# Key parts of an attention block: a buffer of their own for the low parts, fewer key transfers, block sums in smaller steps

## The chip, the core and the metric

The kernel runs on one core of a Trainium2 chip. Its time is the device time of one execution in microseconds (us); the number that counts is the median of several runs. Profiles are of one execution each, and a profiled execution has a time of its own.

Names used below: PE is TensorE, which multiplies matrices (PEld is its loading of weights); DVE is VectorE; ACT is ScalarE; POOL is GpSimd, which here does little but issue transfers; SP issues the other transfers. Each engine works its own list of instructions in order.

## What is computed

The reference is one layer of a generator over 512 latent tokens (an 8 x 64 grid) and 256 context tokens, of width 1024. `h` is the normalised, modulated input, `hc` the same for the context:

```
parts = _split_in(h @ w_in[i])                 # 10 parts of 1024 columns
q = _apply_rope(_heads(parts[4]), cos, sin)    # 16 heads of 64
k = _apply_rope(_heads(parts[5]), cos, sin)
v = _heads(parts[6])
k_c, v_c = ...                                 # hc @ w_in, key and value columns
attn = _neighbourhood_attention(q, k, v, k_c, v_c, rpb[i])
y_a = (silu(z_a) * b_gate * _dwconv3(c_gate * x_in, conv_w, conv_b)) @ w_out_conv
y_b = (silu(z_b) * attn) @ w_out_attn
x = x + gt * _rmsnorm((sigmoid(g_a) * y_a + sigmoid(g_b) * y_b) @ w_o[i], post_g)
```

Each token attends to a window of 8 x 16 latent keys and to all 256 context keys in one softmax.

## The kernel before

**Two parts per number.** Every product is made from float32 operands that are cut in two: a high part `H` (a cast on ACT, line 67) and a low part `L = source - H` (a subtraction on DVE, line 68). The helper `split` does both.

**The stages.** First the input is normalised and modulated into the tiles `h` (high and low part of each of eight 128-row pieces, lines 373 to 500), while the first products run (`steps`, lines 397 to 401). DVE's work there is the conditioning (line 352), `fL` (line 385) and the low parts of `h` (line 68). Convolution units and the context's conditioning follow, to about 117 us of the profile. Then come the keys and queries and the values of the first pair of heads, and then the attention: eight pairs of heads, each with two heads of four blocks, so 64 slots. In each slot the loop (lines 783 on) issues some of the fill work that `plan` lists for this pair (projections for later pairs, `qk`, `v`; convolution units `cx`, `bz`; gates `zb`, `g`), the gathering of the head before (`gather`, line 713 on PE), the scores of the block two slots ahead (`scores`, lines 663 and 672 on PE, 679 on DVE, 685 to 687 on ACT) and, every second slot, the transposes of two blocks (`turn2`, line 694) with the split into `TH` and `TL`. An output stage follows from about 527 us on.

**Products in seven instead of eight.** Some fill items are made by `pair` (lines 268 to 291): 256-column blocks, products at line 262, with sums of blocks in place of blocks. `pair` writes its two results into tiles of the tag `tc`, of which there are three in rotation: first `c1` (copy at line 273), then the second half of `c2` (line 276) and its first half (line 278). The two products after that accumulate into the bank that the copy at line 278 has read. In the pairs of heads 2, 4 and 6 of the plan, the items are `qk`, then `zb` by `pair`, then `cx` by `pair`. `Chunk.first` prepares the next chunk of weights for such an item: sums on DVE at lines 101, 103, 105 and 106, and splits.

**The block sums of h.** `pair` needs sums of blocks of `h`: `S2`, `S3`, `S4`, `X1`. `block_sums` (lines 561 to 579) makes them once, in four steps (k = 0 to 3), each of two tiles `a` and `b` of the tag `tc`: two additions (line 569), two half subtractions (570, 571), two half operations (573) and two splits into `S` tiles. The loop calls `next(sums)` in the slots 4, 6, 9 and 11.

**The keys.** `keys_queries(p)` projects queries and keys of a pair. `keys` (lines 631 to 636) splits the keys into high and low part, once for the 512 latent and once for the 256 context columns. The low part goes into a tile `low`, also of the tag `tc`. Then three transfers on POOL's queue put the parts where the scores need them: high half to the second tile (634), low half to the second tile (635), low half over the high half in the first tile (636, which must wait until 634 has read it). The two tiles `ks` of a pair are for its head 0 and head 1; four buffers hold two pairs.

**What sets the order.** The order of instructions on each engine is set by a scheduler that takes the program's order and puts in what it holds to be ready, as buffers of a tag come free. The first stage is written under a fixed order for its own instructions, but others can stand between them.

Of the kernel before, what the change touches and what calls it, by code (L numbers as in the profile page):

```python
# [10 lines left out]
F32R = mybir.dt.float32r  # L11
# [4 lines left out]
P = 128  # L16
D = 1024
KT = 8
S = 512
C = 256  # L20
# [7 lines left out]
def layer(ctx: ExitStack, tc, xp, ctxt, ctxT, cc, wmod, small, wfirst, win, wout, wo, rel, tab, out):  # L28
    nc = tc.nc
# [4 lines left out]
    cv = ctx.enter_context(tc.tile_pool(name="cv", bufs=2))  # L34
# [29 lines left out]
    def split(H, L, src, scale=None):  # L64

        if scale is None:
            nc.scalar.copy(H, src)  # L67
            nc.vector.tensor_sub(L, src, H.bitcast(F32))  # L68
        else:
            nc.scalar.mul(H, src, scale)  # L70
            nc.vector.scalar_tensor_tensor(
                out=L, in0=src, scalar=scale, in1=H.bitcast(F32), op0=ALU.mult, op1=ALU.subtract
            )
# [91 lines left out]
    def proj_c(ps, w, u):  # L165

        (H, L, _), cs = w, slice(u * P, (u + 1) * P)
        for k in range(KT):
            nc.tensor.matmul(  # L169
                ps, lhsT=H[k][:, cs], rhs=hcs[k].rearrange("p a c -> p (a c)"), start=k == 0, stop=False,  # L170
                skip_group_check=True,
            )
        for k in range(KT):
            nc.tensor.matmul(
                ps[:, :C], lhsT=L[k][:, cs], rhs=hc[0][k], start=False, stop=k == KT - 1, skip_group_check=True
            )

    def summed(ps):
        t = cv.tile([P, S], F32, name="ta")[:, :256]
        nc.scalar.copy(t, ps[:, 256:])  # L180
        nc.vector.tensor_add(t, t, ps[:, :256])
        return t
# [137 lines left out]
    def unit(w, i, m=hx):  # L320
        ps = pj()
        proj_T(ps, w, i, m)
        return ps


    with ExitStack() as p0:
# [17 lines left out]
        cols = {}  # L344
# [204 lines left out]
        ks = [5, 6, 7, 0, 1, 2, 3, 4]  # L549
# [11 lines left out]
    def block_sums():  # L561

        h0, h1 = slice(0, 256), slice(256, S)
        for n in ("S2", "S3", "S4", "X1"):
            blocks_h[n] = [], []
        for k in range(4):
            a, b = (cv.tile([P, S], F32, name="tc", bufs=3) for _ in range(2))
            for x, i in ((a, k), (b, 4 + k)):
                nc.vector.tensor_add(x, hx[0][i].bitcast(F32), hx[1][i].bitcast(F32))
            nc.vector.tensor_sub(b[:, h1], b[:, h1], a[:, h1])  # L570
            nc.vector.tensor_sub(a[:, h1], a[:, h0], a[:, h1])
            for o, x, y in ((a[:, h0], b[:, h1], a[:, h0]), (b[:, h0], a[:, h0], b[:, h0])):
                nc.vector.scalar_tensor_tensor(out=o, in0=x, scalar=-1.0, in1=y, op0=ALU.mult, op1=ALU.subtract)
            for x, names, tag in ((a, ("S2", "S3"), f"u{k}"), (b, ("S4", "X1"), ("a2", "a3", "s0", "s1")[k])):
                t = hp.tile([P, 2, S], F32R, name=f"{names[0]}{k}", tag=tag)
                split(t[:, 0], t[:, 1], x)
                for n, ts in zip(names, (h0, h1)):
                    for y in range(2):
                        blocks_h[n][y].append(t[:, y, ts])
            yield  # L580
# [4 lines left out]
    aw = pa.enter_context(tc.tile_pool(name="aw", bufs=2, reuse_waits="tile"))  # L585
    swap = [(i + 16) % 32 for i in range(32)]
    lo, hi = slice(0, 64), slice(64, P)
# [5 lines left out]
    def rope(ps, turn=0):  # L593
        t1 = cv.tile([P, S], F32, name="ta")
        nc.vector.tensor_mul(t1, ps, cosin[:, 0])
        t2 = cv.tile([P, S], F32, name="tb")
        nc.vector.stream_shuffle(t2, ps, swap)
        nc.vector.tensor_mul(t2, t2, cosin[:, 1])
        if not turn:
            nc.vector.tensor_add(t1, t1, t2)  # L600
            return t1
        t3 = cv.tile([P, S], F32, name="ta")
        nc.vector.tensor_add(t3[:, :S - turn], t1[:, turn:], t2[:, turn:])
        nc.vector.tensor_add(t3[:, S - turn:], t1[:, :turn], t2[:, :turn])
        return t3
# [16 lines left out]
    def keys_queries(p):  # L622
        w = chunk()
        qf = rope(unit(w, 0), 64)
        sc = 0.125
        qd, qe = ([aw.tile([P, S], F32R, name=n, bufs=3) for h in range(2)] for n in ("qd", "qe"))
        split(qd[0], qe[0], qf, sc)
        yield
        ks = [aw.tile([P, S + C], F32R, name="ks", bufs=4) for h in range(2)]

        def keys(src, cols):
            low = cv.tile([P, S], F32R, name="low", tag="tc", bufs=3)[:, :cols.stop - cols.start]
            split(ks[0][:, cols], low, src)
            nc.gpsimd.dma_start(ks[1][lo, cols], ks[0][hi, cols])
            nc.gpsimd.dma_start(ks[1][hi, cols], low[hi])
            nc.gpsimd.dma_start(ks[0][hi, cols], low[lo])

        keys(rope(unit(w, 1)), slice(0, S))
        yield
        ps = pj()  # L640
        proj_c(ps, w, 1)
        keys(summed(ps), slice(S, S + C))
        for t in (qd, qe):
            for o in (lo, hi):
                nc.gpsimd.dma_start(t[1][o], t[0][hi])  # L645
            nc.gpsimd.dma_start(t[0][hi], t[0][lo])
        KQ[p] = qd, qe, ks
        yield
# [41 lines left out]
    def turn2(pts, b, TH, TL):  # L690
        tps = [psT().rearrange("p (c q) -> p c q", c=4) for _ in pts]
        for tp, pt in zip(tps, pts):
            for c in range(4):
                nc.tensor.transpose(tp[:, c], pt[:, c * P:(c + 1) * P], ident)  # L694
        for n, tp in enumerate(tps):
            split(TH[:, b + n], TL[:, b + n], tp)

    def gather(p, h, TH, TL):
        r, q = (lo, hi)[h], (hi, lo)[h]
        if h == 0 and p % 2 == 0:  # L700
            t = hp.tile([P, 2, S], F32, name=f"at{p}", tag=f"a{p // 2 % 2}")
            attn[p], attn[p + 1], attn[p, "both"] = t[:, 0], t[:, 1], t
        o = psO()
        o3 = o.rearrange("p (b q) -> p b q", b=4)

        work = [(4, slice(0, 4), lambda t: t[:, :, 2]), (5, slice(0, 4), lambda t: t[:, :, 3])]
        work.append((0, slice(0, 4, 3), lambda t: t[:, 0:4:3, 0]))
        for k in range(1, 3):
            work.append((k, slice(k - 1, k + 1), lambda t, k=k: t.rearrange("p b c q -> p (b c) q")[:, 4 * k - 3:4 * k + 1:3]))
        work.append((3, slice(2, 4), lambda t: t[:, 2:4, 1]))  # L710
        for n, (kt, dst, src) in enumerate(work):
            for t in (TH, TL):
                nc.tensor.matmul(  # L713
                    o3[:, dst], lhsT=V[p][:, kt, h], rhs=src(t),
                    start=n == 0 and t is TH, stop=n == len(work) - 1 and t is TL,
                )
        tmp = cv.tile([P, S], F32, name="ta")
        nc.scalar.copy(tmp[r], o[q])
        nc.vector.tensor_add(attn[p][r, 64:512], o[r, :448], tmp[r, :448])
        nc.vector.tensor_add(attn[p][r, 0:64], o[r, 448:], tmp[r, 448:])  # L720
# [38 lines left out]
    def chain(*gs):  # L759
        for g in gs:  # L760
            yield from g
# [6 lines left out]
    for g in (keys_queries(0), values(0)):  # L768
        for _ in g:
            pass  # L770
# [13 lines left out]
    pts = {n: scores(*blocks[n]) for n in range(2)}  # L784
    T = None
    sums = block_sums()
    done = 0
    for i, (p, h, b) in enumerate(blocks):
        slot = i % 8
        if slot == 0:  # L790
            items = chain(*(g for g, _ in fill[p]))
            total, done = sum(n for _, n in fill[p]), 0
        if i in (4, 6, 9, 11):
            next(sums)
        upto = -(-total * (slot + 1) // 8)
        while done < upto:
            next(items)
            done += 1
        if T is not None and b == 0:
            gather(*T)  # L800
        if i + 2 < len(blocks):
            pts[i + 2] = scores(*blocks[i + 2])
        if b == 0:
            TH = aw.tile([P, 4, 4, P], F32R, name="TH", bufs=1)
            TL = aw.tile([P, 4, 4, P], F32R, name="TL", bufs=1)
            T = p, h, TH, TL

        if b % 2:
            turn2([pts.pop(i - 1), pts.pop(i)], b - 1, TH, TL)
# [22 lines left out]
    for n, _ in enumerate(chain(merge_gates(2), merge_gates(3))):  # L832
        ks = range(4 * (n % 2), 4 * (n % 2) + 4)
# [205 lines left out]
    for i in range(2):  # L1039
        cols = slice(256 * i, 256 * (i + 1))  # L1040
# [92 lines left out]
```

## Time and profile before

| | us |
|---|---|
| median of 3 runs (725.94 to 729.69) | 726.06 |
| the profiled execution, its time | 731.14 |
| its span, first to last instruction | 729.3 |
| PE busy in the span | 708.0 |
| DVE busy | 586.8 |
| ACT busy | 425.3 |
| POOL busy | 49.9 |

The mean granted TensorE clock of the profiled execution is 0.987. Of a line of the profile, `L68` is line 68 of the kernel, `tc<-h` says what is written and what is read, `x24` how many instructions the line holds, and a bracket such as `[3.18 <-ACT tc L278]` says how long the engine had been idle before and what ended that.

### The profile page before, as it was taken

How to read it: one execution, taken by the hardware profiler on the slowest of the kernel's cores; microseconds unless marked ns; L12 is line 12 of the kernel's file. 1: busy time of each engine (PE TensorE's matmuls, PEld its weight loads, DVE VectorE, ACT ScalarE, POOL GpSimd, SP SyncE). 2: the span in 40 equal slices, each digit the busy share in tenths (PEclk: the TensorE clock that was granted, in tenths of full speed). 3: DMA queues.
4: the chain of work that ended last, by engine and by line, in shares of the span. 5: the costliest groups of instructions: out<-in, count | busy, mean ns of one | idle time of the engine just before them, and what ended most of it. 6: DMA issues, size and time to landing. Idle time of an engine off the chain costs nothing.

```text
span 729.3 us, 11059 instructions
## 1 busy us (share of the span) xinstructions
PE 708.0 (97%) x4052; PEld 621.7 (85%) x4052; DVE 586.8 (80%) x1139; ACT 425.3 (58%) x822; POOL 49.9 (7%) x102
## 2 busy tenths in 40 slices
PE   8999999999899989999899999899999999999996
PEld 5888888888788888898898899899989999988885
DVE  7979999569888877879687699799797765674996
ACT  7575642456476575775675675688774443352663
POOL 0000002030030300301201103000000000000000
PEclk9999999999999999999899999999999999999999
DMA  8986987362260533432553144232543333480013
GB/s 349 407 314 248 295 307 195 95 148 76 73 149 15 139 112 115 91 107 58 130 182 93 34 145 97 72 111 73 191 159 113 116 116 108 139 300 32 30 58 117
DMA packets 36825, 104.06 MB, mean 143 GB/s; under 512 B 4897, under 2 KB 6689, under 8 KB 36770
## 3 DMA queue, kind: packets, MB, share of 16 engines
q1 hardware_dynamic: 28946, 92.20, 36.8%
q0 software_dynamic: 7680, 11.02, 7.2%
q8 instruction: 32, 0.52, 0.3%
q14 instruction: 23, 0.19, 0.1%
q10 hardware_dynamic: 144, 0.13, 0.1%
HBM read 87.07 MB, written 5.24 MB: 127 GB/s over the span
## 4 chain that ended last, share of the span: by engine, by line
PE 59%; DVE 9%; DMA 5%; ACT 2%; issue 1%; POOL 1%; DVEq 0%; ACTq 0%; POOLq 0%; SPq 0%
PE ps L262 17%; PE ps L143 7%; PE ps L145 7%; PE ps L144 7%; PE ps L940 5%; PE ps L156 5%; PE ps L713 4%; DMA ks<-low 3%; PE ps L694 2%; PE ps L161 2%; DVE w L68 2%; PE ps L663 2%; DMA qe<-qe 1%; PE ps L169 1%; DVE TL L68 1%
## 5 line engine op out<-in xcount | busy, mean ns | idle before, releaser
L68 DVE TENSOR_TENSOR w<-raw,w 128x512 fp32r<-128x512 f32 (+1 forms) x170 | 146.1, 867 | 44.1 <-ACT w L67 43.4
L67 ACT CAST w<-raw 128x512 fp32r<-128x512 f32 (+1 forms) x170 | 128.5, 768 | 84.6 <-PE ps L145 31.4
L262 PE MATMUL ps<-S,w 128*128 128x256 f32 x768 | 102.8, 293 | 8.8 <-ACT tc L278 8.8
L262 PEld LDWEIGHTS ps<-S,w 128*128 128x128 f32 x768 | 99.3, 201 | 9.4 <-ACT tc L278 9.4
L143 PE MATMUL ps<-h,w 128*128 128x512 f32 x272 | 106.8, 392 | 0.0
L145 PE MATMUL ps<-h,w 128*128 128x512 f32 x272 | 106.2, 390 | 0.0
L144 PE MATMUL ps<-h,w 128*128 128x512 f32 x272 | 105.9, 389 | 0.0
L262 PE MATMUL ps<-h,w 128*128 128x256 f32 x576 | 75.2, 284 | 0.2 <-DVE g L279 0.2
L262 PEld LDWEIGHTS ps<-h,w 128*128 128x128 f32 x576 | 71.9, 191 | 1.5 <-DVE g L279 0.5
L145 PEld LDWEIGHTS ps<-h,w 128*128 128x128 f32 x272 | 51.1, 188 | 10.8
L143 PEld LDWEIGHTS ps<-h,w 128*128 128x128 f32 x272 | 51.2, 188 | 10.4
L144 PEld LDWEIGHTS ps<-h,w 128*128 128x128 f32 x272 | 51.1, 188 | 10.5
L685 ACT ACTIVATE pt<-ps,m 128x512 f32<-128x512 f32 x64 | 44.2, 691 | 17.8 <-DVE m L679 17.2
L687 ACT ACTIVATE pt<-pt,z 128x512 f32<-128x512 f32 x64 | 45.9, 726 | 9.0 <-DVE z L686 8.8
L67 ACT CAST TH<-ps 128x512 fp32r<-128x512 f32 x64 | 35.4, 587 | 18.5 <-PE ps L694 18.5
L68 DVE TENSOR_TENSOR TL<-ps,TH 128x512 fp32r<-128x512 f32 x64 | 43.1, 681 | 1.6 <-ACT TH L67 1.4
L679 DVE CUSTOM_DVE_ANT_1 ps<-ps,bt 128x512 f32<-128x512 f32 x56 | 38.8, 696 | 4.0 <-PE ps L663 4.0
L694 PE MATMUL ps<-ident,pt 128*128 128x128 f32 x256 | 33.7, 273 | 0.4 <-DVE TL L68 0.4
L645 POOL DMA_DIRECT2D qd<-qd x16 | 8.3, 524 | 356.7 <-issue 239.1
L156 PE MATMUL ps<-w,h 128*128 128x512 f32 x128 | 32.5, 395 | 0.0
L694 PEld LDWEIGHTS ps<-ident,pt 128*128 128x128 f32 x256 | 29.2, 140 | 3.1 <-ACT pt L687 0.9
L713 PE MATMUL ps<-TH,V 128*128 128x256 f32 (+1 forms) x96 | 29.9, 332 | 1.1 <-ACT TH L67 1.1
(247 smaller groups left out, 1377.3 us busy)
## 6 DMA issues: line engine op xcount, KB each, us to landing
raw<-in_win SPq DMA_DIRECT2D x74, 512.0 KB, 4.5
wm<-in_wmod SPq DMA_DIRECT2D x34, 512.0 KB, 6.2
raw<-in_wout SPq DMA_DIRECT2D x16, 512.0 KB, 3.6
bt<-in_rel SPq DMA_DIRECT2D x16, 256.0 KB, 3.3
B<-in_wo SPq DMA_DIRECT2D x8, 512.0 KB, 6.9
fraw<-in_wfirst SPq DMA_DIRECT2D x8, 384.0 KB, 8.5
qd<-qd POOLq DMA_DIRECT2D x24, 128.0 KB, 2.3
qe<-qe POOLq DMA_DIRECT2D x24, 128.0 KB, 3.8
```

Source lines behind the costliest of these rows:

```text
L67: nc.scalar.copy(H, src)
L68: nc.vector.tensor_sub(L, src, H.bitcast(F32))
L143: nc.tensor.matmul(ps, lhsT=H[k][:, cs], rhs=mH[k], start=k == 0, stop=False)
L144: nc.tensor.matmul(ps, lhsT=H[k][:, cs], rhs=mL[k], start=False, stop=False)
L145: nc.tensor.matmul(ps, lhsT=L[k][:, cs], rhs=mH[k], start=False, stop=k == KT - 1)
L156: nc.tensor.matmul(ps, lhsT=mH[k][:, ts], rhs=both[k].rearrange("p a c -> p (a c)"), start=k == 0, stop=False, skip_group_check=True,)
L262: nc.tensor.matmul(ps, lhsT=w[:, x, k], rhs=act[y][k], start=start and k + o == 0, stop=k == 3 and o == 2, skip_group_check=True,)
L679: nc.vector.tensor_tensor_reduce(out=s3, in0=s3, in1=bt[:, e::4 - e][:, 0:2], scale=-1.0, scalar=3.0e38, op0=ALU.add, op1=ALU.min, accum_o ...
L685: nc.scalar.activation(pt, s, AF.Exp, bias=m, scale=-1.0, accum_out=z)
L687: nc.scalar.mul(pt, pt, z)
L694: nc.tensor.transpose(tp[:, c], pt[:, c * P:(c + 1) * P], ident)
L713: nc.tensor.matmul(o3[:, dst], lhsT=V[p][:, kt, h], rhs=src(t), start=n == 0 and t is TH, stop=n == len(work) - 1 and t is TL,)
```

## The change

It does four things. The low parts of the keys get a tile of their own, `lows` (tag `kl`, one buffer, 768 columns), so the tag `tc` holds only block sums and the results of `pair`. The tiles `ks` have three buffers in place of four, so the second tile of a pair takes the buffer of the first tile of the pair before. The three key transfers are made once per pair over all 768 columns, after the context's keys are split, in place of once for each part: three in place of six. And `block_sums` gives way between the sums of a step and their splits, with eight calls in the slots 4, 5, 6, 8, 9, 10, 12, 13 in place of four.

```diff
@@ block_sums
             for o, x, y in ((a[:, h0], b[:, h1], a[:, h0]), (b[:, h0], a[:, h0], b[:, h0])):
                 nc.vector.scalar_tensor_tensor(out=o, in0=x, scalar=-1.0, in1=y, op0=ALU.mult, op1=ALU.subtract)
+            yield
             for x, names, tag in ((a, ("S2", "S3"), f"u{k}"), (b, ("S4", "X1"), ("a2", "a3", "s0", "s1")[k])):
@@ keys_queries
-        ks = [aw.tile([P, S + C], F32R, name="ks", bufs=4) for h in range(2)]
+        ks = [aw.tile([P, S + C], F32R, name="ks", bufs=3) for h in range(2)]
+        lows = aw.tile([P, S + C], F32R, name="kl", bufs=1)
 
         def keys(src, cols):
-            low = cv.tile([P, S], F32R, name="low", tag="tc", bufs=3)[:, :cols.stop - cols.start]
-            split(ks[0][:, cols], low, src)
-            nc.gpsimd.dma_start(ks[1][lo, cols], ks[0][hi, cols])
-            nc.gpsimd.dma_start(ks[1][hi, cols], low[hi])
-            nc.gpsimd.dma_start(ks[0][hi, cols], low[lo])
+            split(ks[0][:, cols], lows[:, cols], src)
 
         keys(rope(unit(w, 1)), slice(0, S))
         yield
         ps = pj()
         proj_c(ps, w, 1)
         keys(summed(ps), slice(S, S + C))
+        nc.gpsimd.dma_start(ks[1][lo], ks[0][hi])
+        nc.gpsimd.dma_start(ks[1][hi], lows[hi])
+        nc.gpsimd.dma_start(ks[0][hi], lows[lo])
@@ the loop over the slots
-        if i in (4, 6, 9, 11):
+        if i in (4, 5, 6, 8, 9, 10, 12, 13):
             next(sums)
```

PE's list stays the same but for one small product. The order of the other engines moves at three places.

**DVE, end of the first stage, before.** The last piece of `h` (`h_89`), the weights of the next chunk (`w<-raw`), then the conditioning of the context (line 352):

```order
L484 TENSOR_TENSOR col_471<-col_471,sp 128x1
L385 TENSOR_TENSOR fL<-fraw,fH 128x768
L487 TENSOR_SCALAR hcv<-sp 128x32
L68 TENSOR_TENSOR h_89<-m,h_89 128x512
L68 TENSOR_TENSOR w<-raw,w 128x4x256 x2
L352 ISA junk,col_677<-wm,cb,bsc_113 128x1024
```

The same place now, where `tc` and `S_1625` are tiles of the block sums:

```order
L484 TENSOR_TENSOR col_471<-col_471,sp 128x1
L571 TENSOR_TENSOR tc<-tc 128x256
L569 TENSOR_TENSOR tc<-h_83 128x512
L385 TENSOR_TENSOR fL<-fraw,fH 128x768
L487 TENSOR_SCALAR hcv<-sp 128x32
L68 TENSOR_TENSOR h_89<-m,h_89 128x512
L573 SCALAR_TENSOR_TENSOR tc<-tc 128x256
L68 TENSOR_TENSOR w<-raw,w 128x4x256 x2
L573 SCALAR_TENSOR_TENSOR tc<-tc 128x256
L68 TENSOR_TENSOR S_1625<-tc,S_1625 128x512
L569 TENSOR_TENSOR tc<-h_87 128x512
L570 TENSOR_TENSOR tc<-tc 128x256
```

Block sums that stood in the slots of the attention now stand from the first stage on: four of the eight rows of line 569, both halves of line 570 and 571 for k = 0 and 1, and one split stand ahead of the first keys; the rest stands between the first keys and the eighth slot.

**DVE, the `zb` item of the pair of heads 2, before.** Sums for the next chunk (lines 101 to 106, `raw`), its splits (`w`), one block's scores (line 679) and the splits `TL` for the gathering:

```order
L101 TENSOR_TENSOR raw<-raw 128x4x128
L106 TENSOR_TENSOR raw<-raw 128x4x128
L68 TENSOR_TENSOR w<-raw,w 128x512
L679 ISA ps,m<-ps,bt 128x512
L679 ISA m 128x1
L68 TENSOR_TENSOR w<-raw,w 128x512
L103 TENSOR_TENSOR raw<-raw 128x4x128
L686 RECIPROCAL z<-z 128x1
L68 TENSOR_TENSOR TL<-ps,TH 128x512
L68 TENSOR_TENSOR w<-raw,w 128x512
L105 TENSOR_TENSOR raw<-raw 128x4x128
L68 TENSOR_TENSOR TL<-ps,TH 128x512
```

The same place now (line 680 is the old 679, 687 the old 686):

```order
L101 TENSOR_TENSOR raw<-raw 128x4x128
L106 TENSOR_TENSOR raw<-raw 128x4x128
L68 TENSOR_TENSOR w<-raw,w 128x512 x2
L103 TENSOR_TENSOR raw<-raw 128x4x128
L680 ISA ps,m<-ps,bt 128x512
L680 ISA m 128x1
L105 TENSOR_TENSOR raw<-raw 128x4x128
L68 TENSOR_TENSOR w<-raw,w 128x512
L687 RECIPROCAL z<-z 128x1
L68 TENSOR_TENSOR TL<-ps,TH 128x512 x2
```

The instructions are the same twelve; both splits `TL` now stand last.

**POOL, the transfers of the second pair of heads, before** (`qd` and `qe` are the parts of the queries):

```order
L645 DMA qd<-qd 64x512 x2
L645 DMA qe<-qe 64x512 x2
L646 DMA qd<-qd 64x512
L634 DMA ks<-ks 64x512
L635 DMA ks<-low 64x512
L646 DMA qe<-qe 64x512
L636 DMA ks<-low 64x512
L634 DMA ks<-ks 64x256
L635 DMA ks<-low 64x256
L636 DMA ks<-low 64x256
```

The same pair now:

```order
L646 DMA qd<-qd 64x512 x2
L646 DMA qe<-qe 64x512 x2
L647 DMA qd<-qd 64x512
L647 DMA qe<-qe 64x512
L641 DMA ks<-ks 64x768
L642 DMA ks<-kl 64x768
L643 DMA ks<-kl 64x768
```

The three key transfers stand behind those of the queries, and no part of the keys goes ahead of the other.

## The prediction, made before the result was known

> **What bounds the kernel now.** I read the page's busy times first, then PE's list of waits, then windows around them.
>
> ```profile
> span 729.3 us, 11059 instructions
> PE 708.0 (97%) x4052; PEld 621.7 (85%) x4052; DVE 586.8 (80%) x1139; ACT 425.3 (58%) x822; POOL 49.9 (7%) x102
> ```
>
> PE is idle for 21 us in all; nothing but PE's own time, its idle time and its clock can move the end by much. Its waits, as engine, line, releaser, then total us, times, longest:
>
> ```profile
> PE ps L262 <- ACT tc L278: 8.8, 3, 3.2
> PE ps L713 <- ACT TH L67: 1.1, 1, 1.1
> PE ps L713 <- DVE TL L68: 0.9, 1, 0.9
> ```
>
> So there are four places: three times a copy into a `tc` tile, once the gathering's splits. The windows that hold them (columns: the window's length, then busy time and count of PE, PEld, DVE, ACT, POOL; PEclk is the granted clock), with a fifth for comparison:
>
> ```profile
> 180.00:200.00 20.00, 18.08 (x80) 14.71 (x80) 16.45 (x36) 10.65 (x21) 0.00 (x0) 0.91 0.24 79
> 250.00:270.00 20.00, 16.82 (x121) 16.18 (x120) 14.83 (x32) 12.08 (x25) 1.88 (x4) 0.91 0.41 112
> 350.00:370.00 20.00, 16.81 (x112) 16.17 (x112) 14.18 (x32) 11.51 (x25) 2.95 (x6) 0.83 0.31 83
> 450.00:470.00 20.00, 17.54 (x128) 16.94 (x127) 15.44 (x33) 13.73 (x31) 3.57 (x7) 0.91 0.39 100
> 500.00:510.00 10.00, 9.59 (x73) 8.80 (x71) 9.51 (x21) 7.34 (x16) 0.00 (x0) 1.00 0.39 131
> ```
>
> Idle in the first four: 1.92 + 3.18 + 3.19 + 2.46 = 10.75 us. After each of them the clock is also low: 0.09 x 20 = 1.8 us three times and 0.17 x 20 = 3.4 us once, 8.8 us together. In the fifth window 0.41 us of idle time costs no clock.
>
> What makes the copy late shows in the timeline of the second place (start, us, engine, line; a bracket is the idle time before):
>
> ```profile
> 248.92 3.04 PE L262 MATMUL ps<-S,w 128*128 128x256 f32 x24
> 249.83 0.53 POOL L634 DMA_DIRECT2D ks<-ks  x1
> ...
> 251.80 0.40 PE L663 MATMUL ps<-ks,qd 128*128 128x512 f32 x1
> ...
> 253.06 1.67 PE L262 MATMUL ps<-h,w 128*128 128x256 f32 x12
> 253.43 0.69 DVE L106 TENSOR_TENSOR raw<-raw 128x512 f32<-128x512 f32 x1 [1.76 <-DMA raw<-in_win]
> ...
> 254.64 0.69 DVE L679 CUSTOM_DVE_ANT_1 ps<-ps,bt 128x512 f32<-128x512 f32 x1
> ...
> 256.90 0.51 POOL L636 DMA_DIRECT2D ks<-low  x1 [5.53 <-DMA ks<-ks]
> 257.21 0.37 ACT L276 COPY tc<-ps 128x256 f32<-128x256 f32 x1 [4.58 <-DMA ks<-low]
> ...
> 257.91 4.50 PE L262 MATMUL ps<-S,w 128*128 128x256 f32 x24 [3.18 <-ACT tc L278]
> ...
> 258.40 0.69 DVE L68 TENSOR_TENSOR w<-raw,w 128x512 fp32r<-128x512 f32 x1 [3.02 <-ACT w L67]
> ...
> 262.20 0.57 PE L713 MATMUL ps<-TH,V 128*128 128x512 f32 x1
> ...
> 263.08 0.40 PE L713 MATMUL ps<-TL,V 128*128 128x512 f32 x1
> ```
>
> The tile that the copy at line 276 wants was a `low` tile, and a key transfer that has still to read such a tile sits in POOL's queue behind another transfer. ACT stands still for 4.58 us; behind its copy are queued the second copy, the weight splits and the `TH` casts, so DVE waits 3.02 us and PE 3.18 us. The 24 products then take 4.50 us in place of 3.04 us: the lost clock is real.
>
> **What goes.** With `lows` in a buffer of its own no copy into `tc` waits for a key transfer. The tile's own list says what such waits come to, and what the block sums cost DVE:
>
> ```profile
> L569 DVE TENSOR_TENSOR tc<-h x8: 676/685/693, 158.7 to 213.4; 128x512 f32<-128x512 f32 x8
> L573 DVE SCALAR_TENSOR_TENSOR tc<-tc x8: 411/418/426, 167.5 to 216.1; 128x256 f32<-128x256 f32 x8
> L68 DVE TENSOR_TENSOR S<-tc,S x8: 672/684/692, 169.4 to 218.0; 128x512 fp32r<-128x512 f32 x8
> L570 DVE TENSOR_TENSOR tc<-tc x4: 396/412/424, 165.2 to 214.3; 128x256 f32<-128x256 f32 x4
> L571 DVE TENSOR_TENSOR tc<-tc x4: 409/418/424, 166.1 to 215.0; 128x256 f32<-128x256 f32 x4
>   DMA ks<-low: 17.8, 6
> ```
>
> The 17.8 us are ACT's copies and DVE's block sums together. The block sums take 8 x 0.685 + 8 x 0.418 + 8 x 0.684 + 4 x 0.412 + 4 x 0.418 = 17.6 us of DVE, 4.4 us per step, all between 158.7 and 218 us. Two steps and their waits lie just ahead of the first place (near 189 us), where the `TL` splits are late by 1.92 us in all. In the new order they stand elsewhere, so this place goes too. Gross gain: 10.75 + 8.8 = 19.55 us.
>
> **What is late next.** At the three `pair` places PE and the splits `TL` meet again. Without the stop PE starts its 24 products at 257.91 - 3.18 = 254.73 us, is through with them 2.88 us later, at 257.6 (at full clock the row after such 24 products starts at 251.80, for a start at 248.92), and wants `TL` at most 0.88 us after that (263.08 - 262.20), at 258.5. DVE cannot start line 106 before 253.43, since that waits for weights from memory. From there, in the new order: line 106, two `w`, line 103, line 105, one `w` and the first `TL` at 0.61 us start to start ((254.64 - 253.43) / 2), the scores' 0.69 and the reciprocal's 0.1. The second `TL` starts at 258.5 and ends at 259.2. PE waits 0.7 us. I price the three places at that, 2.1 us together; the bounds are none and 1.8 us of clock on top of each. The row with 0.41 us of idle time at full clock is the nearest one below, the place with 1.92 us of idle time the nearest above, so I take no lost clock.
>
> A rule speaks to this price. The Trainium skill's page "TensorE: Matmul & The Clock Gate", in the section "Why this matters for your kernels", sets the limit at idle gaps of about 3 us. The trace does not agree: in the first window 1.92 us of idle time in pieces of at most 1.1 us came with a clock of 0.91. By that rule the first and the last place would owe no clock and the gain would be 3.6 us smaller, an estimate of 715 for what comes to 711 below.
>
> **What moves.** Of the 17.6 us, the rows ahead of the first keys (four of line 569, four of 570 and 571, two of 573, one split) are 4 x 0.685 + 2 x 0.412 + 2 x 0.418 + 2 x 0.418 + 0.684 = 5.9 us; 11.7 us stand between there and 150 us. The room for them is DVE's idle time:
>
> ```profile
> 40.00:50.00 10.00, 10.00 (x46) 8.09 (x45) 6.80 (x10) 7.48 (x9) 0.00 (x0) 1.00 0.87 331
> 50.00:120.00 70.00, 70.00 (x313) 57.99 (x312) 67.95 (x112) 34.31 (x65) 1.29 (x3) 1.00 0.76 262
> 120.00:150.00 30.00, 30.00 (x161) 25.87 (x160) 18.40 (x44) 14.74 (x35) 4.98 (x10) 1.00 0.46 116
> ```
>
> 3.2 + 2.05 = 5.25 us up to 120 us, 11.6 us up to 150 us. It nearly fits, with a backlog of about 1 us. Three covers say what a backlog costs. The closest split of weights ends at 93.83 + 1.22 = 95.05 us and PE starts on that chunk at 95.68:
>
> ```profile
> 93.83 1.22 DVE L68 TENSOR_TENSOR w<-raw,w 128x1024 fp32r<-128x1024 f32 x1
> 95.68 0.39 PE L143 MATMUL ps<-h,w 128*128 128x512 f32 x1
> ```
>
> That is 0.6 us; the new order puts one split of weights some rows earlier there, so I price it at nothing. The first pair's keys:
>
> ```profile
> 128.04 1.15 POOL L636 DMA_DIRECT2D ks<-low  x2 [2.28 <-DMA ks<-ks]
> 136.96 0.40 PE L663 MATMUL ps<-ks,qd 128*128 128x512 f32 x1
> ```
>
> Now the last transfer starts after both parts and behind some 3 us more of DVE work, near 131 us, and lands 4.4 us later (row below); the scores want it at 136.96. Nothing is lost, with 1.5 us of cover. And PE turns the first scores only here, 12 us after making them, which covers DVE's lateness in between:
>
> ```profile
> 149.70 1.03 PE L694 MATMUL ps<-ident,pt 128*128 128x128 f32 x8
> ```
>
> **Fewer buffers and transfers.** The second `ks` tile of a pair now takes the first tile of the pair before, which head 0 reads last at 241.69; the transfers into it come with the context's part, near 249.83 us, so 7 us are to spare. Three transfers per pair go; POOL is busy 7%. Both at nothing.
>
> **The sum.** 731.14 - 19.55 + 2.1 = 713.7 us for an execution like the profiled one. The median of the runs, 726.06, lies 5.1 below that execution. If its stops cost as much, it comes to 708.6; if it lies lower because its stops cost less, to 713.7. I take the middle, 711.
>
> **The rivals.** About 0.5% (3.6 us) is what a measurement of this kernel can tell from no change.
>
> *No new wait* (the rows could be read so, since DVE may get its weights earlier): 19.55 off, 706.5 to 711.6, say 708. Against it: line 106 waits for memory, not for ACT.
>
> *DVE stays late.* If `TL` comes as late as now, for work and not for ACT's stop, only the first place is gained: 1.92 + 1.8, 722.3. Against it: the 3.02 us that DVE waits for ACT.
>
> *The moved sums push the weights.* If none of the idle time before 95 us can be used, 5.9 - 0.6 = 5.3 us of wait and 1.8 us of clock come back: 718. For it: DVE is busy 67.95 of 70 us there.
>
> *Slower: a buffer too few.* If the second `ks` tile came free only after head 1, the transfers would wait for this:
>
> ```profile
> 241.69 0.40 PE L672 MATMUL ps<-ks,qe 128*128 128x256 f32 x2
> ...
> 270.73 0.41 PE L672 MATMUL ps<-ks,qe 128*128 128x256 f32 x2
> ...
> 276.16 0.40 PE L663 MATMUL ps<-ks,qd 128*128 128x512 f32 x1
> ...
> ks<-low POOLq DMA_DIRECT2D x16, 128.0 KB, 4.4
> ```
>
> Two transfers in line, 0.5 + 4.4 us each, from 271.1: 280.9 against the next pair's scores at 276.16. 4.7 us and 1.8 us of clock, seven times, is 45 us; less the 17.45 gained, 754. It decides if the buffer's last reader is head 1. Against it: two tiles per pair in a rotation of three put the second on head 0's.
>
> **Chances.** Forecast 0.58; no new wait 0.14; sums push the weights 0.12; DVE stays late 0.08 (half of it within 0.5%); a buffer too few 0.03; something else 0.05 (0.02 faster, 0.02 same, 0.01 slower). Faster: 0.58 + 0.14 + 0.12 + 0.04 + 0.02 = 0.90; same 0.06; slower 0.04. The range, 705 to 721, holds the first three with their bounds.
>
> **What would show it.** Right: no wait of line 276 for a key transfer; full clock from 50 to 500 us; waits of PE for `TL` at line 713 of about 0.7 us in three places; block sums from the first stage to 150 us. Wrong: PE waits before 150 us; a clock below 0.95 in the three places; PE waiting at line 664 (the scores) for `ks`.

## The result, and the profile after

The kernel after takes 715.11 us (median of 4 runs, 714.70 to 715.67). Before, timed beside it, takes 726.43 us (4 runs, 725.94 to 729.69). The ratio is 0.9835, 95% interval 0.9805 to 0.9865: 1.65% faster, inside the predicted range and 4.1 us above the predicted 711. The profiled execution took 715.21 us with a span of 713.4 us, 15.93 us less than the profiled execution before (731.14). From line 574 on each line number is one higher than before (713 is now 714, 663 is 664), except for the key transfers (636 is 643). Of two kernels further down, one execution each (3977.04 and 3976.95 us) is left out of the medians; nothing on record shows why these two took so long.

The page's head:

```profile
span 713.4 us, 11043 instructions
PE 699.3 (98%) x4052; PEld 614.0 (86%) x4052; DVE 585.3 (82%) x1139; ACT 425.2 (60%) x822; POOL 37.6 (5%) x78
```

PE is busy for 8.7 us less, with the same products: that is half-clock time that is gone, but for 0.94 us in the first 20 us (busy 15.45 us in place of 16.39), which gain nothing, as the wait at line 397 shows. Its idle time fell from 21.3 to 14.1 us. The list of PE's waits (total us, times, longest), without the one at the very start (line 445, 3.3 us, before 3.5):

```profile
PE ps L714 <- DVE TL L68: 2.4, 3, 0.9
PE ps L397 <- ACT h L67: 1.1, 1, 1.1
PE ps L695 <- DVE TL L68: 0.8, 1, 0.8
```

No stop for line 278 is left. The wait of 1.1 us at line 397 is not in before's profile but costs nothing: PE had finished its work ahead of it sooner, and line 397 starts at 15.39 us before and at 15.40 us after. It does not come from the change either: before's second profile, taken for the first experiment, has it with 1.2 us. The windows at the four places, and the two early ones:

```profile
180.00:200.00 20.00, 20.00 (x107) 17.19 (x106) 15.22 (x35) 10.08 (x20) 2.04 (x4) 1.00 0.30 91
244.00:264.00 20.00, 19.19 (x154) 18.44 (x153) 17.86 (x39) 14.67 (x32) 2.04 (x4) 1.00 0.52 143
340.00:360.00 20.00, 19.07 (x152) 18.34 (x152) 17.91 (x39) 15.34 (x33) 2.04 (x4) 1.00 0.51 133
440.00:460.00 20.00, 19.37 (x155) 18.63 (x155) 17.77 (x39) 14.99 (x34) 1.29 (x3) 1.00 0.52 138
...
50.00:120.00 70.00, 70.00 (x313) 58.02 (x312) 69.02 (x112) 36.30 (x68) 0.34 (x1) 1.00 0.77 261
120.00:150.00 30.00, 30.00 (x160) 25.87 (x160) 27.68 (x67) 16.93 (x39) 4.39 (x9) 1.00 0.47 120
```

The clock is full in all of them. DVE is busy 69.02 of 70 us and 27.68 of 30 us where the block sums now stand, and PE has no idle time there. The second place in the timeline:

```profile
247.90 0.37 ACT L278 COPY tc<-ps 128x256 f32<-128x256 f32 x1 [0.97 <-PE ps L262]
249.39 0.69 DVE L106 TENSOR_TENSOR raw<-raw 128x512 f32<-128x512 f32 x1 [1.83 <-DMA raw<-in_win]
250.47 3.04 PE L262 MATMUL ps<-S,w 128*128 128x256 f32 x24
251.26 0.51 POOL L643 DMA_DIRECT2D ks<-kl  x1 [4.75 <-DMA ks<-ks]
253.35 0.40 PE L714 MATMUL ps<-TH,V 128*128 128x512 f32 x1
253.69 1.27 DVE L68 TENSOR_TENSOR TL<-ps,TH 128x512 fp32r<-128x512 f32 x2
255.01 0.50 PE L714 MATMUL ps<-TL,V 128*128 128x512 f32 x1 [0.81 <-DVE TL L68]
```

The last key transfer still starts late (251.26 us, after 4.75 us of waiting for the one before it), but the copy at line 278 no longer waits for it; it runs at 247.90 us, as soon as PE has made its operand. What is left is the predicted wait: line 106 waits for weights from memory, the `TL` splits stand behind it, and PE waits 0.81 us for the second one.

**Where the time comes from.** PE runs the same products in nearly the same order, so its start times tell it place by place. Before, the timeline has:

```profile
194.30 0.40 PE L143 MATMUL ps<-h,w 128*128 128x512 f32 x1
...
365.17 0.40 PE L663 MATMUL ps<-ks,qe 128*128 128x512 f32 x1
365.40 0.40 PE L713 MATMUL ps<-TL,V 128*128 128x512 f32 x1
...
465.62 0.39 PE L663 MATMUL ps<-ks,qe 128*128 128x512 f32 x1
465.85 0.40 PE L713 MATMUL ps<-TL,V 128*128 128x512 f32 x1
...
510.18 0.63 PE L694 MATMUL ps<-ident,pt 128*128 128x128 f32 x4 [0.36 <-DVE TL L68]
```

After, the same instructions:

```profile
190.24 0.39 PE L143 MATMUL ps<-h,w 128*128 128x512 f32 x1
...
351.21 0.39 PE L664 MATMUL ps<-ks,qe 128*128 128x512 f32 x1
352.53 0.50 PE L714 MATMUL ps<-TL,V 128*128 128x512 f32 x1 [0.93 <-DVE TL L68]
...
448.70 0.39 PE L664 MATMUL ps<-ks,qe 128*128 128x512 f32 x1
449.73 0.50 PE L714 MATMUL ps<-TL,V 128*128 128x512 f32 x1 [0.63 <-DVE TL L68]
...
494.32 0.63 PE L695 MATMUL ps<-ident,pt 128*128 128x128 f32 x4 [0.76 <-DVE TL L68]
```

Up to the first place the two run level (0.01 us apart at line 397, 0.07 us at line 145 just ahead of the first place). The lead is 194.30 - 190.24 = 4.06 us after the first place. At the second it is 262.20 - 253.35 = 8.85 when PE comes to the gathering, and 263.08 - 255.01 = 8.07 after the wait for `TL`. At the third it is 13.96 and then 12.87, at the fourth 16.92 and then 16.12; at 494 us it is 15.86. So:

| place | gain predicted | gain measured | `TL` predicted | `TL` measured |
|---|---|---|---|---|
| near 189 us | 3.72 | 4.06 | - | - |
| near 253 us | 4.98 | 4.79 | 0.7 | 0.78 |
| near 352 us | 6.59 | 5.89 | 0.7 | 1.09 |
| near 449 us | 4.26 | 4.05 | 0.7 | 0.80 |
| near 494 us | - | - | - | 0.26 |
| sum | 19.55 | 18.79 | 2.1 | 2.93 |

18.79 - 2.93 = 15.86 us, all but 0.07 us of the difference of the two executions.

### The profile page after: what moved, and what is told of

Its sections match the earlier page's. It is cut to its first block, busy times and chain, and to the rows that moved or that the text cites. A ratio compares the mean times of both kernels' runs of the same rounds, so it can differ in the third digit from the quotient of the medians.

```text
span 713.4 us, 11043 instructions
## 1 busy us (share of the span) xinstructions
PE 699.3 (98%) x4052; PEld 614.0 (86%) x4052; DVE 585.3 (82%) x1139; ACT 425.2 (60%) x822; POOL 37.6 (5%) x78
## 4 chain that ended last, share of the span: by engine, by line
PE 89%; DVE 6%; DMA 3%; ACT 1%; issue 1%; DVEq 0%; SPq 0%; ACTq 0%
PE ps L262 17%; PE ps L143 13%; PE ps L144 13%; PE ps L145 13%; PE ps L156 6%; PE ps L941 5%; PE ps L714 4%; PE ps L695 3%; PE ps L161 3%; PE ps L664 2%; DMA raw<-in_win 2%; PE ps L169 2%; DVE w L68 2%; PE ps L397 2%; PE ps L401 2%; PE ps L398 2%
## 5 line engine op out<-in xcount | busy, mean ns | idle before, releaser
L262 PE MATMUL ps<-S,w 128*128 128x256 f32 x768 | 97.4, 283 | 0.0
L262 PEld LDWEIGHTS ps<-S,w 128*128 128x128 f32 x768 | 94.5, 192 | 0.0
L686 ACT ACTIVATE pt<-ps,m 128x512 f32<-128x512 f32 x64 | 44.1, 689 | 15.2 <-DVE m L680 14.1
L714 PE MATMUL ps<-TL,V 128*128 128x256 f32 (+1 forms) x96 | 28.2, 323 | 2.4 <-DVE TL L68 2.4
```

The costliest lines, as they stand in the source:

```text
L262: nc.tensor.matmul(ps, lhsT=w[:, x, k], rhs=act[y][k], start=start and k + o == 0, stop=k == 3 and o == 2, skip_group_check=True,)
L686: nc.scalar.activation(pt, s, AF.Exp, bias=m, scale=-1.0, accum_out=z)
L714: nc.tensor.matmul(o3[:, dst], lhsT=V[p][:, kt, h], rhs=src(t), start=n == 0 and t is TH, stop=n == len(work) - 1 and t is TL,)
```

## The experiments

Theory: the low parts stood in `tc` buffers until slow key transfers had read them, and every one of the four places came from an instruction that waited for such a buffer. Rivals: the number and the time of the key transfers; the smaller steps and the new place of the block sums. Eleven kernels, before itself among them, ran in three sets, each beside before on the same chip; before's medians there were 727.66 (19 runs), 726.76 (23) and 727.59 us (7). Where a kernel has added lines, the numbers behind them shift by as many: 714 of after is 716 or 717 there, 695 is 697 or 698.

**Before once more.** No edit.

> The kernel before, unchanged, for the clock of its ordinary runs and a second profile. In its first profile (731.14 us, span 729.3) the clock was 0.987 and the low-clock time after the four places came to about 9 us; the median of its runs was 726.4. Theory (the stops are always there, and the clock time that each one costs varies from one execution to the next): 726, mean clock of the ordinary runs above 0.987, about 0.993, spans near 724.5; PE's idle time at line 262 for line 278 again 8 to 9 us in three stops. Rival (the stops themselves are shorter in ordinary runs): clock 0.987 and a span near 724.5.

Measured: 727.38 us (nine runs, 725.49 to 729.12), clock from 0.987 to 0.996. PE's waits in its profile (729.12 us, clock 0.993):

```profile
PE ps L262 <- ACT tc L278: 8.5, 3, 3.2
PE ps L713 <- DVE TL L68: 2.7, 3, 0.9
```

The three stops come to nearly the same as in the first profile (8.8 us there). The clock doesn't: 0.993 in place of 0.987. And where the clock stays full behind a stop, PE comes to `TL` earlier and waits for it: 2.7 us against 0.9. So the rival (shorter stops) falls. Beside the second set, before ran from 724.16 us at a clock of 0.996 to 731.11 us at 0.987: 0.009 x 727 = 6.5 us of clock for 6.95 us of time. But these are the two ends: over all runs of before in the three sets, the time goes with the clock and yet runs of one clock differ, at 0.994 from 724.78 to 728.69 us. So the clock that its stops cost makes part of before's spread, and where the rest comes from stays open. After has 0.997 to 0.999 in all runs, and in its profile the missing part lies behind 710.95 us, when PE has no more work. My theory said 0.993 and spans near 724.5 for ordinary runs; the clock was right, the spans were 723.6 to 727.3.

**The buffer alone.**

```diff
-        ks = [... name="ks", bufs=4) ...]
+        ks = [... name="ks", bufs=3) ...]
+        lows = aw.tile([P, S + C], F32R, name="kl", bufs=1)
-            low = cv.tile([P, S], F32R, name="low", tag="tc", bufs=3)[:, :cols.stop - cols.start]
+            low = lows[:, cols]
```

> Before with one edit: the low parts of the keys in a buffer of their own (and ks in three buffers, to pay for it). Six key transfers per pair and block sums in four steps as before. Theory (the shared buffers alone make all four places): as the kernel after, 715 (713.5 to 717), no wait for line 276, PE's waits for TL 0.6 to 1.1 us in the three places, and the block sums from the first stage to 150 us. Rival one (six transfers in POOL's queue are what is late): 726, with waits for the key transfers left. Rival two (the eight steps are what lets the block sums move up): 719, the place near 189 us comes back with its 3.9 us, the other three are gone.

Measured: 715.07 us (714.60 to 715.58), ratio 0.9828 (0.9811 to 0.9844). Its waits and its first block sums, from two views:

```profile
PE ps L714 <- DVE TL L68: 1.7, 3, 0.7
...
PE ps L695 <- DVE TL L68: 0.6, 1, 0.6
```

```profile
L569 DVE TENSOR_TENSOR tc<-h x8: 684/686/692, 21.7 to 135.9; 128x512 f32<-128x512 f32 x8
```

This edit has the whole gain. Both rivals fall: three transfers in place of six are worth nothing that shows here, and the eight steps are not what lets the block sums move up; free `tc` buffers do that. The edit has three `ks` buffers too; the next kernel keeps those and gains nothing, so they alone are not the cause.

**Everything but the buffer.**

```diff
-        lows = aw.tile([P, S + C], F32R, name="kl", bufs=1)
+        lows = []
-            split(ks[0][:, cols], lows[:, cols], src)
+            low = cv.tile([P, S], F32R, name="low", tag="tc", bufs=3)[:, :cols.stop - cols.start]
+            split(ks[0][:, cols], low, src)
+            lows.append((cols, low))
-        nc.gpsimd.dma_start(ks[1][hi], lows[hi])
-        nc.gpsimd.dma_start(ks[0][hi], lows[lo])
+        for cols, low in lows:
+            nc.gpsimd.dma_start(ks[1][hi, cols], low[hi])
+            nc.gpsimd.dma_start(ks[0][hi, cols], low[lo])
```

> After, with the low parts back in two tiles of the tag tc (so the transfers from low parts are made per part: five transfers per pair, all after the context's part); eight steps of block sums and three ks buffers stay. Theory: the copies into tc wait for key transfers again and the block sums stand late again: 726 (724 to 732), three stops of PE for line 278 of about 3 us. Rival (late, fewer transfers and eight steps are what helped): 715 to 719.

Measured: 728.03 us (721.94 to 732.18), ratio 1.0003 (0.9976 to 1.0030): nothing is left of the gain. The profiled execution is its fastest, 721.94 us. PE's waits there, and the block sums' row with the `tc` tiles' waits for transfers:

```profile
PE ps L262 <- ACT tc L276: 5.1, 3, 2.7
PE ps L717 <- ACT TH L67: 2.0, 3, 1.2
```

```profile
L569 DVE TENSOR_TENSOR tc<-h x8: 667/685/693, 158.6 to 214.3; 128x512 f32<-128x512 f32 x8
...
  DMA ks<-low: 11.8, 4
```

The stops are back (in two pieces: 5.1 and 2.0 us, of at most 2.7; I expected three whole ones), the block sums are late again, and this execution lost no clock (0.998). Its other runs did, down to 0.985, and took up to 10.2 us longer.

**Block sums held back.**

```diff
+    late = [None]
             for x, i in ((a, k), (b, 4 + k)):
+                nc.vector.tensor_copy(x[:, 0:1], late[0])
                 nc.vector.tensor_add(x, hx[0][i].bitcast(F32), hx[1][i].bitcast(F32))
...
+            late[0] = pts[i][:, 0:1]
             next(sums)
```

> After, with the block sums held back: ahead of each of the eight additions DVE copies one column (128x1) of the newest softmax tile into the tc tile, so no addition can start before the attention has come that far; low parts keep their own buffer. Theory (two separate effects: moved sums are worth the place near 189 us, the own buffer is worth the other three): 719 (718 to 721), waits of PE for TL near 189 us of about 2 us with lost clock, the three places as in the kernel after. Rival one (the sums' new place is worth nothing, the place near 189 us went for another reason): 715 to 716. Rival two (the three stops came from the sums and the low parts together): above 722.

Measured: 715.41 us (714.86 to 715.90). The additions, now line 572, and PE's waits, from two views:

```profile
L572 DVE TENSOR_TENSOR tc<-h x8: 681/689/694, 158.8 to 205.7; 128x512 f32<-128x512 f32 x8
```

```profile
PE ps L717 <- DVE TL L68: 2.6, 3, 1.2
...
PE ps L698 <- DVE TL L68: 0.9, 1, 0.9
```

My theory falls: the block sums stand where they stood before, and the place near 189 us does not come back. Moving them up is worth nothing. Before's timeline has what stood there with them:

```profile
163.90 0.69 DVE L569 TENSOR_TENSOR tc<-h 128x512 f32<-128x512 f32 x1 [3.19 <-DMA ks<-low]
...
166.89 0.69 DVE L569 TENSOR_TENSOR tc<-h 128x512 f32<-128x512 f32 x1 [0.36 <-DMA ks<-low]
```

DVE stood still for 3.55 us, since an addition wanted a `tc` tile that a key transfer had still to read. All of DVE's work behind that should be late by it, `TL` at 189 us too. The next kernel tests this.

**The rotation kept, the transfers' reading gone.** To the kernel with the buffer alone:

```diff
             low = lows[:, cols]
+            dummy = cv.tile([P, S], F32R, name="low", tag="tc", bufs=3)
+            nc.vector.tensor_copy(dummy[:, 0:1], src[:, 0:1])
```

> The low parts in a buffer of their own with six transfers and four steps of block sums, but keys still takes a tile of the tag tc for each part, in which DVE writes one column (128x1) and which no transfer reads. So the order in which tc buffers come round is that of before and the block sums stand late again, from some 158 us on; only the transfers' reading is gone. Theory: the three stops for line 278 stay away, since no copy waits for a transfer; the place near 189 us tells what it was: 715 to 716 if it was the waiting of DVE and ACT for tc buffers, 719 with PE's waits for TL near 189 us if it was the block sums' work as such. Rival (the number of tc tiles in rotation is what makes the stops, whoever reads them): 722 to 726.

Measured: 713.13 us (713.01 to 713.64), ratio 0.9819 (0.9789 to 0.9848). Its block sums and its waits, from two views:

```profile
L569 DVE TENSOR_TENSOR tc<-h x8: 673/683/693, 157.0 to 204.9; 128x512 f32<-128x512 f32 x8
```

```profile
PE ps L697 <- DVE TL L68: 0.5, 1, 0.5
PE ps L716 <- DVE TL L68: 0.3, 1, 0.3
```

The block sums run in the same order of `tc` buffers as before and just as late, and PE has no wait near 189 us. So it was the waiting, not the work. That the kernel is some 2 us faster than after (timed in another set, where before is 0.3 us slower) was not expected; its second place shows a reason:

```profile
250.86 0.68 DVE L106 TENSOR_TENSOR raw<-raw 128x512 f32<-128x512 f32 x1
...
252.74 1.27 DVE L68 TENSOR_TENSOR TL<-ps,TH 128x512 fp32r<-128x512 f32 x2
```

The order on DVE is another one: the scores' instruction, two splits `w` and line 103 now stand ahead of line 106, which no longer waits for memory, and `TL` starts at 252.74 us in place of 253.69. That the scheduler chose this order because other buffers were free at other times is argued, not shown, and the order was not tried by itself.

**The waits that are left: `TL` first.** After, with:

```diff
+        if b == 3:
+            turn2([pts.pop(i - 1), pts.pop(i)], b - 1, TH, TL)
         upto = -(-total * (slot + 1) // 8)
...
-        if b % 2:
+        if b == 1:
             turn2([pts.pop(i - 1), pts.pop(i)], b - 1, TH, TL)
```

> After, with the transposes and the TH/TL splits of a head's last two blocks written ahead of the fill work of their slot, not behind it, so that on DVE the TL splits stand ahead of the block sums of the next weights. Theory (the waits left in the three places are TL standing behind weights' sums that wait for memory): those waits, 2.5 us in all, go and nothing takes their place: 712.5 (712 to 713.5). Rival (the softmax tiles are not ready that early, and PE then waits at the transposes for ACT's line 688): 715 to 720, with waits of PE at line 698 or ahead of it for pt.

Measured: 713.45 us (712.72 to 713.73), ratio 0.9820 (0.9791 to 0.9849). PE's waits from 14 to 520 us:

```profile
PE ps L714 <- DVE TL L68: 0.7, 1, 0.7
PE ps L714 <- ACT TH L67: 0.7, 1, 0.7
```

The three waits for `TL` are gone, and the two left are new, at 489 and 507 us in the last pair of heads. The 2.4 and 0.8 us of after became 1.4: 1.8 us less, 1.7 us by time (715.11 and 713.45 are from different sets), where I expected 2.6. What stays late at the three places is therefore the place of `TL` in DVE's list, as the prediction had it.

**Both together.** The kernel with the kept rotation, with `turn2` first except in the last pair of heads:

```diff
+        early = b == 3 and p < NPAIR - 1
+        if early:
+            turn2([pts.pop(i - 1), pts.pop(i)], b - 1, TH, TL)
         upto = -(-total * (slot + 1) // 8)
...
-        if b % 2:
+        if b % 2 and not early:
```

> The kernel of e9_rotation_only (713.1), with the transposes and the TH/TL splits of a head's last two blocks ahead of the fill work of their slot, as in e8_turn_first (713.45), except in the last pair of heads, where that cost 0.7 us of waiting for TL at 489 us and as much for TH. Theory (both took away the same waits, TL behind the weights' sums, so little is left): 712.5 to 713.2, PE's waits for TL between 200 and 470 us zero. Rival (they are independent gains): 711.5.

Measured: 712.43 us (712.03 to 712.86), ratio 0.9797 (0.9768 to 0.9825), the fastest kernel here. Of PE's waits between 20 and 520 us one is left:

```profile
PE ps L697 <- DVE TL L68: 0.5, 1, 0.5
```

The two edits took away the same waits, as the theory said; its 712.5 to 713.2 us lie next to the measured median, and the rival's 711.5 did not come.

**A stop without a transfer.** After, with extra copies on ACT in the three gate pairs (18, 13 or 9 in place of N):

```diff
-            nc.scalar.copy(c2[:, second], e)
+        for _ in range(extra):
+            nc.scalar.copy(c2[:, first], e)
+        nc.scalar.copy(c2[:, second], e)
...
-            yield from pair(*z)
+            yield from pair(*z, N)
```

> After, with 18 extra copies on ACT (128x256, 0.27 us start to start as two such copies in a row in before) ahead of the copy at line 276, in the three gate pairs alone: a stop of the same place and about the same size as before, with no transfer in it. Cover that has to be used up first: 2.2 us, from the end of the copy at line 278 to PE's use. Theory (the stop alone makes the loss, and clock is lost on top by chance, 0 to 3.4 us each): three stops of 18 x 0.27 - 2.2 = 2.7 us, and 0 to 1.7 us of clock in most executions: 723 to 729, with runs spread over several us as in before (724.8 to 731.4). Rival (the clock is lost by something else than the stop, such as transfers): 722 to 723.5 with a spread below 1.5 us and full clock.

Measured: 727.23 us (726.50 to 728.74), clock 0.992 to 0.994; so three stops that ACT makes by itself, with no transfer in them, cost as much as the four places of before, clock too. They were larger than the 2.7 us I reckoned, and in pieces, since the scheduler put other ACT work between the copies; PE's waits (line 675 is the second half of the scores, which wait for the softmax tile `pt`):

```profile
PE ps L675 <- ACT pt L688: 4.6, 3, 1.5
PE ps L262 <- ACT tc L278: 3.3, 3, 1.6
```

I was wrong about the spread: 2.2 us, not several. The clock was lost in every run, about the same amount.

> As the one with 18 extra copies, with 13. Stops of 13 x 0.27 - 2.2 = 1.3 us. Theory (clock is lost after stops of about 2 to 3 us, as in before, and not after 0.8 to 1.0 us, as in after): 718 to 719.5, a spread below 1.5 us, clock 0.997 or more. Rival (1.3 us is enough): 720 to 725, with a spread of several us.

Measured: 723.80 us (721.54 to 727.46), clock 0.988 to 0.998. The stops came out larger than the 1.3 us I reckoned: PE waits 4.6 us at line 675 and 2.3 us for `TH`, up to 2.5 us per place. So my 718 to 719.5 is wrong, and the time lies in the rival's range, but the rival is not shown by it: no stop of 1.3 us was made. Two of its windows:

```profile
244.00:264.00 20.00, 17.46 (x122) 16.04 (x122) 14.68 (x34) 17.55 (x44) 2.04 (x4) 0.91 0.39 102
340.00:360.00 20.00, 17.41 (x124) 15.54 (x124) 15.83 (x38) 17.82 (x46) 3.98 (x8) 1.00 0.63 147
```

The idle time is the same in both, 2.54 and 2.59 us, and so are its two pieces (0.92 and 1.53 us, 0.97 and 1.54 us); one place lost clock and the other didn't. The last section shows in what they differ.

> After, with 9 extra copies on ACT in the three gate pairs (18 gave 727.2, 13 gave 723.8 with runs from 721.5 to 727.5). With 13, PE's waits in each place came in two pieces, up to 1.1 us for TH and 1.5 us for the softmax tile. Theory (it is the idle time close together, not the longest single piece, that costs clock): with 9 copies about 1.1 us less of it, 1 to 1.8 us per place, no clock lost in most executions: 717 to 720 with a spread below 2 us. Rival (any stop beyond the waits of the kernel after costs clock): 721 and more, spread of several us.

Measured: runs of 716.79, 717.98 and 718.95 us, with clocks of 0.998, 0.998 and 0.995. PE's waits in the execution of 717.98 us, at full clock:

```profile
PE ps L262 <- ACT tc L278: 3.4, 3, 1.1
PE ps L716 <- ACT TH L67: 1.4, 3, 0.6
```

That is 1.4 to 1.7 us per place, in two pieces. Two of three runs lost no clock, as the theory said; the spread of 2.2 us is just beyond the 2 us that it allowed.

**A buffer too few.**

```diff
-        ks = [... name="ks", bufs=3) ...]
+        ks = [... name="ks", bufs=2) ...]
```

> After, with two buffers for the tiles ks in place of three, so that the second tile of a pair takes the one that head 1 of the pair before reads last. The prediction priced this: transfers land 4.7 us after the scores want them, plus 1.8 us of clock, seven times, 45 us: 760 from 715. Theory: waits of PE at line 664 for ks in seven places, 745 to 765. Rival (the scores of the next pair come late enough, or other work fills the time, so that two buffers are enough): below 722.

Measured, one run: 745.90 us, clock 0.983. PE's wait, and its first row in the timeline:

```profile
PE ps L664 <- DMA ks<-kl: 22.9, 5, 7.0
```

```profile
276.41 0.80 PE L664 MATMUL ps<-ks,qd 128*128 128x512 f32 x1 [6.39 <-DMA ks<-kl]
```

So the rival's mechanism is real and its condition is the one that the prediction named: with three buffers there is no such wait, with two there are five. It costs 30.8 us against after, where 45 were reckoned: five places, not seven.

Not tried: four `ks` buffers beside the new one, and the eight steps alone.

## Why the prediction was right, and where its number was off

- **The cause.** Right. The buffer alone gives 715.07, everything but the buffer 728.03.
- **Three places at `pair`.** Right in kind and in size: gains of 4.79, 5.89 and 4.05 us where 4.98, 6.59 and 4.26 were written. The 6.59 of the place near 352 us counts some time twice: the clock was low there from 358.16 to 364.99 us, and PE stood idle in the first 1.01 us of that (the products start at 359.17). So the lost clock is 0.5 x (6.83 - 1.01) = 2.9 us, not 3.4, and with the stop of 3.19 us that makes 6.1.
- **The first place, "so this place goes too".** It went, for 4.06 us, and the waits that the sentence names were the cause. That the steps "stand elsewhere" was not the cause: with the steps late (715.41 and 713.13) the place stays away.
- **The wait for `TL`, 0.7 us each.** Right in mechanism and place, low in size: 0.78, 1.09 and 0.80 us, and 0.26 more at 494 us, which was not in the sum. No clock was lost on them, as chosen. Taking the three away brought 1.7 us net.
- **Moved block sums, priced at nothing.** Right; DVE filled up to 69.02 of 70 us and PE waited for nothing there. The same holds for transfers and for the third `ks` buffer.
- **From the execution to the median.** This step failed. The sum for an execution like the profiled one was 713.7, and came to 715.2: gains 0.76 lower, `TL` 0.83 higher. The text then took 711, half way to 708.6, for the case that the stops of ordinary runs cost as much as the profiled one's. They don't: the profiled execution had lost nearly the most clock of all runs of before (0.987, with runs from 0.984 to 0.997), and a lower median before meant that there was less to gain. The kernel after has no such loss to spare: its profiled execution (715.21) stands at its median (715.11).
- **The rule on idle gaps.** In before one stop of 2.46 us came with a clock of 0.91, in the kernel with 13 copies two idle pieces of 0.92 and 1.53 us, within 3 us, did so too, and in the kernel without the buffer one stop of 2.67 us came at full clock. The Trainium skill's page "TensorE: Matmul & The Clock Gate" sets the limit at about 3 us, in "Why this matters for your kernels"; the runs do not agree with it as the least length of a single gap: shorter stops, and pieces close together, can cost clock, and whether they do depends on where they lie (last section). That the estimate made by that rule, 715, is what was measured is luck: it leaves the first and the last place without lost clock, and these gave 4.06 and 4.05 us, where their idle time alone is 1.92 and 2.46.
- **Rivals.** No new wait (708; the middle of its bounds, 706.5 and 711.6, is 709): PE waits 2.4 us for `TL`, so no. DVE stays late (722.3): no, the three places are gone but for these waits. Moved sums push the weights (718): no, PE is never idle from 20 to 150 us; its only waits before that lie in the first 16 us, and before's profiles have them too. A buffer too few: only with two.

## What to carry to other kernels

A tile that a queued transfer has still to read should not share its rotation with tiles that compute engines need: the engine that wants the next buffer stands still, in order, with all that is queued behind it. Look for the releaser of a wait to see the buffer, and for the first engine that stood still, even 25 us ahead of where PE stops. If stops cost clock in some executions and not in others, measure how runs spread before a gain is scaled from one profile, and take the gain from the sum without the clock as the floor.

## What was not expected of the hardware

**When idle time costs clock.** It looks like chance: in one kernel, places with 2.54 and 2.59 us of idle time had a clock of 0.91 and 1.00, and the fourth place of before lost clock for a stop of 2.46 us in one profile and none for 2.52 us in the other. Windows that begin and end where the clock changes show more. While PE has work, the low clock (0.50) comes in stretches of 3.41 us, or two of them in a row, and within one execution all of them begin on one grid of 3.41 us steps: in before's first profile at 190.91, 259.17, 358.16 and 460.56 us, which are 20, 29 and 30 steps apart. What tells the cases apart is PE's idle time within one step:

| kernel, place | step of the grid, us | PE idle in it, us | clock in the next step |
|---|---|---|---|
| before, first profile, second place | 255.76 to 259.17 | 2.15 | 0.50 |
| before once more, second place | 253.05 to 256.46 | 1.70 | 1.00 |
| the same stop, its other part | 256.46 to 259.87 | 1.03 | 1.00 |
| before, first profile, fourth place | 457.15 to 460.56 | 2.25 | 0.50 |
| before once more, fourth place | 454.43 to 457.85 | 1.32 | 1.00 |
| the same stop, its other part | 457.85 to 461.26 | 1.20 | 1.00 |
| 13 copies, second place | 251.58 to 254.99 | 2.01 | 0.50 |
| 13 copies, third place | 350.57 to 353.98 | 1.28 | 1.00 |
| the same pieces, the rest | 353.98 to 357.39 | 1.31 | 1.00 |

A stop costs clock when enough of it falls into one step, and a stop of the same length that a border of the grid cuts into two smaller parts does not. The grid lies elsewhere in each execution (full clock is first on record at 13.41 us in before's first profile, at 10.70 us in its second), so for the program it is chance. In the thirteen traces, up to PE's last work, every step at full clock with 1.88 us or more of idle time is followed by a low one, and every one with 1.54 us or less by a full one; between them 1.61 us cost clock once (18 copies) and 1.70 us did not, twice. This is read from the traces, and no kernel was made to move a stop over a border on purpose. Pieces of up to 0.93 us cost none in after (0.997 to 0.999 in all runs); 1.4 to 1.7 us in two pieces cost some in one of three runs, 2.5 us in two pieces in most, and with 18 copies each of 12 runs lost about the same.

**Lost clock hides waits.** Where clock is lost, PE arrives later at what it would have waited for next, so part of the loss is hidden: 0.9 us of waiting for `TL` at a clock of 0.987, 2.7 us at 0.993.
